# V of all four head pairs as one product of 512 columns, in two passes over the contraction

## The chip, the cores and the metric

The kernel runs on one core of a Trainium2 chip. The metric is device time in microseconds (us) of one execution, the median of three runs. The engines named below are TensorE (PE, with its weight loads PEld), VectorE (DVE), ScalarE (ACT), GpSimd (POOL) and SyncE (SP). Each takes its own instructions strictly in order and waits for the others by semaphores. DMA transfers are issued from the queues of SP and ACT.

## The reference

One decoder layer over 2048 positions of 1024 channels, in float32. Its first step is a projection of x; the rest is attention, a state-space branch (S5), gates, an output projection and a layer norm.

```python
proj = jnp.einsum('bld,de->ble', h, w_in[layer])
q, k, v   # 3 groups x 8 heads x 64 each, = 1536 columns each
z_a, u_s, z_s   # 512 columns each
gate_logits     # 2048 columns
attn = _dilated_mixture(q, k, v)        # per group: band of 128 keys back, dilation 1, 4, 16
attn = attn * silu(z_a);  y_a = attn @ w_attn_up
y = gelu(_s5(u_s, ...)); y = y * sigmoid(y @ w_glu + b_glu) * silu(z_s); y_s = y @ w_ssm_up
out = (sigmoid(g_a) * y_a + sigmoid(g_s) * y_s) @ w_o
h = layer_norm(ALPHA * h + out)
```

## The kernel before

Every float32 product is made of three products of parts: x and each weight are split into a high part (a cast to fp32r, "hi") and the rest ("lo"), and hi·hi, hi·lo and lo·hi are summed in PSUM. So one block of 128 output channels over 1024 positions is 8 tiles of the contraction x 2 halves of the positions x 3 = 48 matmuls of 512 columns. The sequence is done in two halves of 1024 positions (h = 0, 1).

**Weights.** `Weights` walks along a list of weight tiles, 128 x 1024 each. `fetch` issues the load of a tile (on ACT's queue, L137). `ahead` and `ahead2` are called inside the block that uses the tile before: they split the next tile in two parts of 512 columns, hi by a cast on ACT (L172), lo by a subtraction on POOL (L175; for some later tiles on DVE), and fetch the one after it. `take` hands a tile to its block.

**Jobs.** A job is one head pair (of four) in one of three groups. `job_proj` makes its V, Q and K; Q and K are one block each (`xgemm`, L215). V is made for two head pairs at once, in jobs of even pairs: `v_gemm` (L431 on) has x as the stationary operand and 256 weight columns as the moving one, 192 matmuls (L446). Two groups of four tiles of positions use two PSUM banks of the tag `proj`; the first half of the contraction is done for all four tiles, then the second half with the second weight tile. Each full bank is copied to SBUF by ACT (L414, tile `th`) and stored to DRAM (`vD`, L415). The job of the odd pair finds its V there.

**Attention.** `job_attn` (L534 on) is a chain over eight tiles of positions. One step has scores on PE (L595, L597), a sum with the bias and a row extreme on DVE (L602), exponentials on ACT (L606), transposes of the tile before on PE (L614), their split by ACT (L616) and DVE (L617), the product with V of the tile before that (L625), and sums by ACT (L630), DVE (L632) and POOL (L633).

**Order.** The instructions stand in the order in which the program writes them. `interleave` runs the projections of the next job (the bulk, in units of six matmuls) beside the attention of the last one (the side), each at its share of a given total. A bulk is counted in blocks of 48 matmuls of 512 columns: four blocks for a job with V, three for a job of an odd pair (Q, K and one further block, za or zs). The four u blocks stand at the start of each half.

Of the kernel before, what the change touches and what calls it, by code (L numbers as in the profile page):

```python
# [41 lines left out]
def layer_kernel(ctx, tc, xT, xnat, w_in, w_v, w_up, w_glu, w_o, bglu, lng, lnb,  # L42
# [30 lines left out]
    vD = [[[dram.tile([HALF, 256], F32, name=f"vD{h}{p}{g}") for g in range(3)] for p in range(2)] for h in range(2)]  # L73
# [49 lines left out]

    class Weights:
# [14 lines left out]
        def load_first(self, i, k):  # L139
            c = self.cols(i, k)  # L140
            S.dma_start(self.raws[i][0][:, c], self.plan[i][:, c])
# [13 lines left out]
        def begin(self):  # L155
            raw, n = self.raws[len(self.splits)]
            left = len(self.plan) - len(self.splits)
            if left <= 4:
                hi, lo = (mpbox["mp"].tile([128, HALF], F32R, name=f"w{n_}", tag=f"m{2 * left - 1 - k_}")
                          for k_, n_ in enumerate(("hi", "lo")))  # L160
            else:
                hi = wp.tile([128, HALF], F32R, name="whi", tag="whi", bufs=2)
                lo = wp.tile([128, HALF], F32R, name="wlo", tag="wlo", bufs=2)
            self.splits.append((hi, lo))
            self.part(0)

        def part(self, k, i=None):
            i = len(self.splits) - 1 if i is None else i
            hi, lo = self.splits[i]
            raw = self.raws[i][0]  # L170
            c = self.cols(i, k)
            A.copy(hi[:, c], raw[:, c])  # L172

            def low(eng):
                eng.tensor_tensor(lo[:, c], raw[:, c], hi[:, c].bitcast(F32), op=OP.subtract)  # L175
# [99 lines left out]
    def first_blocks(load, evac):  # L275
# [22 lines left out]
        for kt, blk in order:  # L298
            if blk == 0 and kt < 7:
                next(load)  # L300
            if (kt, blk) == (0, 0):
                for i in range(2):
                    wts.part(1, i)
            mms(blk, kt)
            if (kt, blk) == (2, 1):
                wts.fetch(4)
            yield 6 * 0.216
            if (kt, blk) == (7, 0):
                wts.ahead()
                wts.finish()  # L310
                for t in range(2):
                    evac[0](t, ps[0][t])
# [51 lines left out]
    def job_proj(ap, wts, h, pair, g):  # L364
# [9 lines left out]
        odd = pair % 2  # L374
        vd = vD[h][pair // 2][g]

        def load_v():

            c = slice(128 * odd, 128 * odd + 128)
# [51 lines left out]
    def v_gemm(evac):  # L431
        w = [wts.take(), None]
        wts.ahead()
        for grp in range(2):
            ps = [ps_tile("proj", 2).rearrange("t (i c) -> t i c", i=2) for _ in range(2)]
            for half_k in range(2):
                if grp == 0 and half_k == 1:
                    w[1] = wts.take()
                for t in range(4):
                    o = ps[t // 2][:, t % 2]  # L440
                    for k4 in range(4):
                        kt = 4 * half_k + k4
                        wc = slice(k4 * 256, (k4 + 1) * 256)
                        for n, (m, wx) in enumerate((("h", 0), ("h", 1), ("l", 0))):
                            i = 4 * grp + t
                            T.matmul(o, X[m, kt][:, 128 * i:128 * i + 128], w[half_k][wx][:, wc],  # L446
                                     start=kt == 0 and n == 0 and t % 2 == 0, stop=kt == 7 and n == 2,
                                     skip_group_check=True)
                    if (grp, half_k) in ((0, 0), (1, 1)):
                        if t == 0:  # L450
                            wts.ahead()
                            if grp == 0:
                                wts.finish()
                        if t == 1:
                            wts.ahead2()
                    if half_k and t % 2:
                        evac(2 * grp + t // 2, ps[t // 2])
                    yield 6 * 0.216
# [215 lines left out]
    def u_evac(h, b):  # L674
        def ev(t, ps):
            ut = wp.tile([128, 512], F32, name="th", tag="th", bufs=2)
# [15 lines left out]
    def z_block(dst, outer=False):  # L692
# [5 lines left out]
        def ev(t, ps):  # L698
            zt[t] = wp.tile([128, 512], F32, name="th", tag="th", bufs=2)
# [7 lines left out]
    def gate_block(h, d, outer=False, early=False):  # L707
        box = {}

        def ev(t, ps):  # L710
            cols = slice(t * 512, (t + 1) * 512)
            if early:
                zt = wp.tile([128, 512], F32, name="th", tag="th", bufs=2)
# [9 lines left out]

    plan = []
    for h in range(2):
        plan += [w_in[40 + b] for b in range(4)]
        for pair in range(NPAIR):
            for g in range(3):
                if pair % 2 == 0:
                    plan += [w_v[pair // 2, g, k] for k in range(2)]  # L730
                plan += [w_in[12 * m + g * 4 + pair] for m in range(2)]
                if pair % 2:
                    plan.append((w_in[36 + pair - 1], w_in[44 + pair // 2], w_in[36 + pair])[g])
# [225 lines left out]
    with tc.tile_pool(name="ap", bufs=1) as ap:  # L959
        ub = [u_block(0, b) for b in range(2, 4)]  # L960
        interleave(chain([first_blocks(first_x(ap), [u_evac(0, b) for b in range(2)])] + ub
                         + [job_proj(ap, wts, 0, 0, 0)]), 8 * BLK, s5_tables(ap), 32.0)
        table_store.pop()()
        pend = None
        for h in range(2):
            bulk = [u_block(1, b, b == 0) for b in range(4)] if h else []
            n = len(bulk)
            for pair in range(NPAIR):
                for g in range(3):
                    if h or pair or g:  # L970
                        bulk.append(job_proj(ap, wts, h, pair, g))
                        n += 2 if pair % 2 else 4
                    if pair % 2:
                        bulk.append(zs_block(h, pair // 2) if g == 1 else za_block(h, pair - 1 + g // 2))
# [3 lines left out]
                    else:  # L978
                        interleave(chain(bulk), n * BLK, pend, 16.0, 12 * 0.216 if g == 0 and pair % 2 else 0.0)
# [273 lines left out]
    def stage_glu(h, sact, stile, zs):  # L1253
        late = []

        def ev_e(e, box):
            def ev(t, ps):
# [3 lines left out]
                th = wp.tile([128, 512], F32, name="th", tag="th", bufs=2)  # L1261
# [359 lines left out]
def host_layout(inp):  # L1621
# [11 lines left out]
    wv = a["w_in"][0][:, 3072:4608].reshape(2, 4, 128, 3, 2, 256)  # L1633
    d["w_v"] = c(wv.transpose(4, 3, 0, 2, 1, 5).reshape(2, 3, 2, 128, 1024))
# [40 lines left out]
```

## Time and profile before

| | |
|---|---|
| median of three runs | 2167.19 us (2167.11 to 2167.34) |
| the profiled execution's own time | 2166.73 us |
| its span, first to last instruction | 2164.9 us |
| PE busy | 2137.0 us, 99% |
| DVE, ACT, POOL busy | 55%, 47%, 33% |
| granted TensorE clock, mean | 0.998 |

A line of the profile names the engine, the line of the program, the operation, what it writes and reads, and its duration. Matmuls overlap: each is shown for longer than the time to the next one's start, so rates are read from starts that follow each other. In brackets stands how long the engine was idle before, and which instruction it waited for.

### The profile page before, as it was taken

How to read it: one execution, taken by the hardware profiler on the slowest of the kernel's cores; microseconds unless marked ns; L12 is line 12 of the kernel's file. 1: busy time of each engine (PE TensorE's matmuls, PEld its weight loads, DVE VectorE, ACT ScalarE, POOL GpSimd, SP SyncE). 2: the span in 40 equal slices, each digit the busy share in tenths (PEclk: the TensorE clock that was granted, in tenths of full speed). 3: DMA queues.
4: the chain of work that ended last, by engine and by line, in shares of the span. 5: the costliest groups of instructions: out<-in, count | busy, mean ns of one | idle time of the engine just before them, and what ended most of it. 6: DMA issues, size and time to landing. Idle time of an engine off the chain costs nothing. (4 is left out here: it accounts for less than half of the span.)

```text
span 2164.9 us, 32185 instructions
## 1 busy us (share of the span) xinstructions
PE 2137.0 (99%) x11440; PEld 1822.8 (84%) x11440; DVE 1191.7 (55%) x3062; ACT 1007.4 (47%) x2355; POOL 704.2 (33%) x589
## 2 busy tenths in 40 slices
PE   8999999999999999999999999999999999999998
PEld 7998889998888999889998888888888878888786
DVE  7644554445553244554445654258887784358725
ACT  3355665556554355665555665233433352232222
POOL 2322253253342234243243252410100014322643
PEclk9999999999999999999999999999999999999999
DMA  6333344343374333434344344554345363533721
GB/s 177 112 98 96 108 127 128 95 127 118 104 233 97 97 99 122 124 108 113 97 130 117 106 108 119 175 169 142 112 141 166 124 208 127 159 114 118 261 88 78
DMA packets 227568, 278.12 MB, mean 128 GB/s; under 512 B 89552, under 2 KB 175440, under 8 KB 227408
## 3 DMA queue, kind: packets, MB, share of 16 engines
q10 hardware_dynamic: 91776, 143.81, 21.7%
q1 hardware_dynamic: 135632, 132.25, 20.6%
q8 instruction: 91, 1.49, 0.3%
q14 instruction: 69, 0.57, 0.1%
HBM read 189.24 MB, written 74.19 MB: 122 GB/s over the span
## 5 line engine op out<-in xcount | busy, mean ns | idle before, releaser
L215 PE MATMUL proj<-xh,whi 128*128 128x512 f32 x1600 | 645.1, 403 | 1.2 <-ACT gt L719 1.2
L215 PE MATMUL proj<-xh,wlo 128*128 128x512 f32 x1600 | 628.2, 393 | 0.0
L215 PE MATMUL proj<-xl,whi 128*128 128x512 f32 x1600 | 625.8, 391 | 0.0
L175 POOL TENSOR_TENSOR wlo<-wraw,whi 128x512 fp32r<-128x512 f32 (+1 forms) x268 | 357.1, 1343 | 530.7 <-ACT whi L172 508.9
L215 PEld LDWEIGHTS proj<-xh,wlo 128*128 128x128 f32 x1600 | 300.2, 188 | 65.5
L215 PEld LDWEIGHTS proj<-xh,whi 128*128 128x128 f32 x1600 | 301.4, 188 | 54.6 <-issue 1.5
L215 PEld LDWEIGHTS proj<-xl,whi 128*128 128x128 f32 x1600 | 301.2, 188 | 51.3
L606 ACT ACTIVATE Sx<-Sx,st 128x256 f32<-128x256 f32 (+1 forms) x384 | 181.3, 473 | 263.8 <-DVE st L602 254.9
L633 POOL TENSOR_TENSOR og<-ot 128x128 f32<-128x128 f32 x192 | 88.1, 459 | 532.7 <-DVE ot L632 516.4
L172 ACT CAST whi<-wraw 128x512 fp32r<-128x512 f32 (+1 forms) x328 | 194.7, 617 | 116.5 <-PE ob L1406 43.2
L617 DVE TENSOR_TENSOR PT<-tr,PT 128x512 fp32r<-128x512 f32 (+1 forms) x192 | 118.9, 619 | 219.9 <-ACT PT L616 219.7
L446 PE MATMUL proj<-whi,xh 128*128 128x256 f32 x768 | 220.8, 287 | 0.0
L446 PE MATMUL proj<-wlo,xh 128*128 128x256 f32 x768 | 218.1, 284 | 0.9 <-POOL wlo L175 0.8
L446 PE MATMUL proj<-whi,xl 128*128 128x256 f32 x768 | 217.1, 283 | 0.0
L446 PEld LDWEIGHTS proj<-wlo,xh 128*128 128x128 f32 x768 | 146.7, 191 | 2.9 <-POOL wlo L175 2.4
L446 PEld LDWEIGHTS proj<-whi,xl 128*128 128x128 f32 x768 | 146.7, 191 | 0.0
L446 PEld LDWEIGHTS proj<-whi,xh 128*128 128x128 f32 x768 | 146.6, 191 | 0.1
L602 DVE CUSTOM_DVE_ANT_0 Sx<-sca,bias 128x256 f32<-128x256 f32 (+1 forms) x192 | 74.6, 389 | 105.3 <-PE sca L597 101.8
L632 DVE TENSOR_TENSOR ot<-ob,ot 64x256 f32<-64x256 f32 x192 | 81.0, 422 | 83.3 <-ACT ot L630 71.7
L632 DVE TENSOR_TENSOR ot<-oa,ot 64x256 f32<-64x256 f32 x192 | 81.1, 422 | 75.1 <-ACT ot L630 61.9
L614 PE MATMUL tr<-ident,Sx 128*128 128x128 f32 x664 | 110.0, 276 | 5.7 <-ACT Sx L606 5.1
L400 DVE TENSOR_TENSOR KC<-proj,KC 64x512 fp32r<-64x512 f32 x96 | 66.1, 689 | 82.9 <-ACT KC L398 81.6
(319 smaller groups left out, 3778.9 us busy)
## 6 DMA issues: line engine op xcount, KB each, us to landing
wraw<-in_w_in_dram ACTq DMA_DIRECT2D x102, 512.0 KB
ld<-gD SPq DMA_DIRECT2D x32, 512.0 KB
gD<-gt ACTq DMA_DIRECT2D x27, 512.0 KB
wraw<-in_w_v_dram ACTq DMA_DIRECT2D x24, 512.0 KB
vD<-th ACTq DMA_DIRECT2D x48, 256.0 KB
cB<-coefD SPq DMA_DIRECT2D x48, 256.0 KB
VV<-vD SPq DMA_DIRECT2D x16, 512.0 KB
xr<-in_xT_dram SPq DMA_DIRECT2D x16, 512.0 KB
```

The costliest lines, as they stand in the source:

```text
L172: A.copy(hi[:, c], raw[:, c])
L175: eng.tensor_tensor(lo[:, c], raw[:, c], hi[:, c].bitcast(F32), op=OP.subtract)
L215: T.matmul(ps, w[:, wc], m(kt)[:, cols], start=kt == 0 and n == 0, stop=3 * kt + n == last)
L400: V.tensor_tensor(gdst(lo, g, t), gsrc(ps[rows[s]], g), gdst(hi[rows[s]].bitcast(F32), g, t), op=OP.subtract)
L446: T.matmul(o, X[m, kt][:, 128 * i:128 * i + 128], w[half_k][wx][:, wc], start=kt == 0 and n == 0 and t % 2 == 0, stop=kt == 7 and n == 2, ...
L602: V.tensor_tensor_reduce(sx[:, s, lo:], ps2[s][:, lo:256], bias[:, s, lo:], scale=-0.125, scalar=3.0e38, op0=OP.add, op1=OP.min, accum_out ...
L606: A.activation(sx[:, s, lo:], sx[:, s, lo:], AF.Exp, scale=-1.0, bias=st[:, 0, s, c:c + 1], accum_out=st[:, 1, s, c:c + 1])
L614: T.transpose(p3[:, s, b], Sx[i][:, s, b * 128:(b + 1) * 128], ident)
L617: V.tensor_tensor(PT[:, 1, :, pos], p3[:, :, lo:], PT[:, 0, :, pos].bitcast(F32), op=OP.subtract)
L632: V.tensor_tensor(ot[half[s]], O[half[s], s], ot[half[s]], op=OP.add)
L633: P.tensor_tensor(og[pair, g][:, i * 128:(i + 1) * 128], ot[:, 0], ot[:, 1], op=OP.add)
```

## The change

V of a group is now made for all four head pairs at once, in the jobs of pair 0: 512 weight columns are the moving operand, and one matmul does what two did. A weight tile now holds two tiles of the contraction instead of four, so a V product needs four weight tiles. It goes in two passes, each over half the contraction: in pass 0 each group of two position tiles is copied to `th` by ACT and stored to DRAM; in pass 1 that sum is loaded again, added to the bank by DVE and stored. These stores and loads are issued by SP. The two PSUM banks of a group are now filled alternately and both are full at the group's end.

Weight tiles are held in pieces of 512 columns: three pieces of raw weights instead of two tiles of 1024, four pieces each of hi and lo as before in bytes. Each piece has its own load. `th` has three buffers instead of two. The first two weight tiles lie in a tile that V uses later.

Of the four u blocks of half 0, two remain at the start (u2 and u3 go beside attention); of those of half 1, one remains. za, zs and u blocks now stand one by one in the jobs of pairs 1 to 3 by the table `BESIDE`; only job (3, 1) of half 0 has none.

```diff
-                raw = wp.tile([128, HALF], F32, name="wraw", tag="wraw", bufs=2)
-                if len(self.raws) > 2:
-                    A.dma_start(raw[:, :n], src)
+                raw = Split()
+                for p in range(2):
...
+                        raw.tiles[p] = wp.tile([128, 512], F32, name="wraw", tag="wraw", bufs=3)
+                        A.dma_start(raw.tiles[p], src[:, 512 * p:512 * p + 512])
...
-        def ev_v(b, ps):
-            vs = wp.tile([128, 512], F32, name="th", tag="th", bufs=2).rearrange("k (i c) -> k i c", i=2)
-            A.copy(vs, ps)
-            A.dma_start(vd[256 * b:256 * b + 256].rearrange("(i k) c -> k i c", i=2), vs)
-        if not odd:
-            yield from v_gemm(ev_v)
+        if not pair:
+            yield from v_gemm(vd)
...
+        def load(grp):
+            for tt in range(2 * grp, 2 * grp + 2):
+                S.dma_start(tile_of(tt), rows(tt))
+        for p in range(2):
+            w = [wts.take(), None]
+            wts.ahead()
+            if p:
+                load(0)
+            for grp in range(4):
+                ps = [ps_tile("proj", 2) for _ in range(2)]
+                for k4 in range(4):
+                    if grp == 0 and k4 == 2:
+                        w[1] = wts.take()
+                    wc = slice(512 * (k4 % 2), 512 * (k4 % 2) + 512)
+                    for t in range(2):
+                        i = 2 * grp + t
+                        for n, (m, wx) in enumerate((("h", 0), ("h", 1), ("l", 0))):
+                            T.matmul(ps[t], X[m, 4 * p + k4][:, 128 * i:128 * i + 128], w[k4 // 2][wx][:, wc],
+                                     start=k4 == 0 and n == 0, stop=k4 == 3 and n == 2)
+                    if (grp, k4) == (0, 0):
+                        wts.finish()
+                    if (grp, k4) == (0, 1):
+                        wts.ahead2()
+                    if grp == 3 and k4 == 0:
+                        wts.ahead()
+                    if grp == 3 and k4 == 1:
+                        wts.ahead2()
+                    if k4 == 3:
+                        for t in range(2):
+                            tt = 2 * grp + t
+                            if p:
+                                V.tensor_tensor(vs[tt], ps[t], vs[tt], op=OP.add)
+                            else:
+                                A.copy(tile_of(tt), ps[t])
+                            S.dma_start(rows(tt), vs[tt])
+                        if p and grp < 3:
+                            load(grp + 1)
                     yield 6 * 0.216
...
+    BESIDE = {(1, 0): "a0", (1, 1): "u2", (1, 2): "s0", (2, 0): "a1", (2, 1): "u3", (2, 2): "s1", (3, 0): "a2",
+              (3, 2): "a3"}
+    extra = [BESIDE, {**BESIDE, (3, 1): "u1"}]
+    front = [2, 1]
```

On PE, at the start of the V product of job (0, 1) of half 0, before the change: behind the scores stand 48 matmuls with the first weight tile (whi_1049), two groups of 12 in bank proj_1144 and two in proj_1145, then the second weight tile (whi_1140).

```order
L597 MATMUL scb_1122<-KC_603,QLb0_600 128x128
L446 MATMUL proj_1144<-whi_1049,xh0_191 128x256
...
L446 MATMUL proj_1145<-whi_1049,xh0_191 128x256
...
L614 MATMUL tr_1209<-ident_71,Sx_1127 128x128 x2
L446 MATMUL proj_1144<-whi_1140,xh4_275 128x256
L446 MATMUL proj_1144<-wlo_1141,xh4_275 128x256
```

The same place on PE after the change (whi_1022 and whi_1038 are the two pieces of the first weight tile, whi_1117 is the first piece of the second):

```order
L639 MATMUL scb_1099<-KC_391,QLb0_388 128x128
L480 MATMUL proj_1121<-whi_1022,xh0_186 128x512
L480 MATMUL proj_1121<-wlo_1023,xh0_186 128x512
L480 MATMUL proj_1121<-whi_1022,xl0_187 128x512
L480 MATMUL proj_1122<-whi_1022,xh0_186 128x512
...
L480 MATMUL proj_1122<-whi_1038,xl1_203 128x512
L480 MATMUL proj_1121<-whi_1117,xh2_238 128x512
L480 MATMUL proj_1121<-wlo_1118,xh2_238 128x512
```

The second weight tile is now the 13th matmul instead of the 49th, and the second bank the 4th instead of the 25th.

On ACT, at the same place before the change: the casts of the last K block, the exponentials of the first attention step, then both hi casts of the second weight tile.

```order
L398 CAST KC_603<-proj_1079 64x4x128 x2
L606 ACTIVATE Sx_1127,st_1118<-Sx_1127,st_1118 128x128 x2
L172 CAST whi_1140<-wraw_1067 128x512 x2
L137 DMA wraw_1172<-in_w_in_dram 128x1024
```

And after it:

```order
L425 CAST KC_391<-proj_1056 64x4x128 x2
L648 ACTIVATE Sx_1104,st_1095<-Sx_1104,st_1095 128x128 x2
L198 CAST whi_1117<-wraw_1042 128x512
L198 CAST whi_1129<-wraw_1044 128x512
L153 DMA wraw_1139<-in_w_v_dram 128x512
L153 DMA wraw_1141<-in_w_v_dram 128x512
```

The hi casts stand at the same place on ACT as before; only what needs them on PE has moved.

On DVE, at the end of the first group of pass 1 of the same V product, after the change (before, no V work stood on DVE): the sums of an attention step (sca_1379, scb_1380), the split of its transposes (tr_1390), then the two adds that empty the banks proj_1351 and proj_1352. "ISA" is what the profile calls CUSTOM_DVE_ANT_0.

```order
L644 ISA Sx_1385,st_1095<-sca_1379,bias_1092 128x256
...
L659 TENSOR_TENSOR PT_1096<-tr_1390,PT_1096 128x2x256
L494 TENSOR_TENSOR th_1347<-proj_1351,th_1347 128x512
L494 TENSOR_TENSOR th_1349<-proj_1352,th_1349 128x512
```

On PE there, the scores and the transposes stand ahead of the last unit of six, and the next group (proj_1411, in the bank of proj_1351) follows directly:

```order
L637 MATMUL sca_1379<-KC_391,QA_385 128x256
...
L656 MATMUL tr_1390<-ident_71,Sx_1302 128x128 x4
L480 MATMUL proj_1351<-whi_1359,xh7_333 128x512
...
L480 MATMUL proj_1411<-whi_1278,xh4_278 128x512
```

## Rows read from the trace of the kernel before

**Rows 1.** The page: busy us (share of the span) and instructions of engines.

```profile
PE 2137.0 (99%) x11440; PEld 1822.8 (84%) x11440; DVE 1191.7 (55%) x3062; ACT 1007.4 (47%) x2355; POOL 704.2 (33%) x589
```

**Rows 2.** The page, one of V's three product groups: count, busy, mean ns, idle.

```profile
L446 PE MATMUL proj<-wlo,xh 128*128 128x256 f32 x768 | 218.1, 284 | 0.9 <-POOL wlo L175 0.8
```

**Rows 3.** Timeline of PE: start, us, engine, line; steady stretches of both products.

```profile
31.11 0.39 PE L215 MATMUL proj<-xh,whi 128*128 128x512 f32 x1
33.83 0.39 PE L215 MATMUL proj<-xh,whi 128*128 128x512 f32 x1
...
57.30 0.28 PE L446 MATMUL proj<-wlo,xh 128*128 128x256 f32 x1
60.90 0.28 PE L446 MATMUL proj<-wlo,xh 128*128 128x256 f32 x1
```

**Rows 4.** Timeline, start of the V product of job (0, 1), half 0.

```profile
97.90 1.18 ACT L398 CAST KC<-proj 64x512 fp32r<-64x512 f32 x2 [3.20 <-PE proj L215]
98.09 0.33 PE L446 MATMUL proj<-whi,xh 128*128 128x256 f32 x1
99.11 1.39 DVE L400 TENSOR_TENSOR KC<-proj,KC 64x512 fp32r<-64x512 f32 x2 [4.03 <-ACT KC L398]
102.18 1.13 ACT L172 CAST whi<-wraw 128x512 fp32r<-128x512 f32 x2
102.92 2.56 POOL L175 TENSOR_TENSOR wlo<-wraw,whi 128x512 fp32r<-128x512 f32 x2 [3.74 <-issue]
104.50 0.37 PE L446 MATMUL proj<-whi,xh 128*128 128x256 f32 x1
```

**Rows 5.** Timeline, three other V products: PE's first matmul, POOL's lo.

```profile
52.87 0.28 PE L446 MATMUL proj<-whi,xh 128*128 128x256 f32 x1
55.00 2.58 POOL L175 TENSOR_TENSOR wlo<-wraw,whi 128x512 fp32r<-128x512 f32 x2 [6.33 <-ACT whi L172]
...
750.91 0.28 PE L446 MATMUL proj<-whi,xh 128*128 128x256 f32 x1
755.99 2.54 POOL L175 TENSOR_TENSOR wlo<-wraw,whi 128x512 fp32r<-128x512 f32 x2 [6.10 <-ACT whi L172]
...
807.49 0.28 PE L446 MATMUL proj<-whi,xh 128*128 128x256 f32 x1
813.07 2.53 POOL L175 TENSOR_TENSOR wlo<-wraw,whi 128x512 fp32r<-128x512 f32 x2 [2.58 <-issue]
```

**Rows 6.** Timeline, end of a u block that fills both banks alternately.

```profile
667.58 0.58 ACT L678 COPY th<-proj 128x512 f32<-128x512 f32 x1 [0.34 <-PE proj L215]
667.84 0.40 PE L215 MATMUL proj<-xh,wlo 128*128 128x512 f32 x1
668.22 0.50 PE L215 MATMUL proj<-xh,whi 128*128 128x512 f32 x1
```

**Rows 7.** Timeline, scores and transposes in a row in an attention step.

```profile
131.47 0.28 PE L595 MATMUL sca<-KC,QA 128*128 128x256 f32 x1
131.95 0.60 PE L614 MATMUL tr<-ident,Sx 128*128 128x128 f32 x4
133.50 0.56 ACT L616 CAST PT<-tr 128x512 fp32r<-128x512 f32 x1
134.09 0.69 DVE L617 TENSOR_TENSOR PT<-tr,PT 128x512 fp32r<-128x512 f32 x1 [1.29 <-ACT PT L616]
```

**Rows 8.** Windows, attention (0,0) beside four blocks, (1,0) beside three: us, busy.

```profile
97.70:153.70 56.00, 56.00 (x382) 51.59 (x381) 24.27 (x67) 30.71 (x77) 17.02 (x19) 1.00 0.27 81
250.70:295.50 44.80, 44.75 (x238) 37.32 (x237) 26.70 (x77) 28.47 (x74) 15.99 (x16) 1.00 0.31 87
```

**Rows 9.** Timeline of PE: the matmuls behind the longest wait.

```profile
1769.54 0.79 PE L215 MATMUL proj<-yh,whi 128*128 128x512 f32 x1 [4.18 <-ACT th L1263]
1770.56 0.63 PE L215 MATMUL proj<-yh,wlo 128*128 128x512 f32 x1
1770.98 0.63 PE L215 MATMUL proj<-yh,whi 128*128 128x512 f32 x1
```

More of the change, by code (lines that the diff above doesn't have):

```diff
@@ L72, in layer_kernel @@
     tabD = dram.tile([128, 1472], F32, name="tabD")
-    vD = [[[dram.tile([HALF, 256], F32, name=f"vD{h}{p}{g}") for g in range(3)] for p in range(2)] for h in range(2)]
+    vD = [[dram.tile([HALF, 512], F32, name=f"vD{h}{g}") for g in range(3)] for h in range(2)]
     zaD = [[dram.tile([128, HALF], F32, name=f"zaD{h}{p}") for p in range(NPAIR)] for h in range(2)]
@@ L121, in next_x, with __init__, __getitem__ @@
         split_x(7, raws[7])
+    class Split:
+        def __init__(self):
+            self.tiles = {}
+        def __getitem__(self, key):
+            rows, c = key
+            p = c.start // 512
+            return self.tiles[p][rows, c.start - 512 * p:c.stop - 512 * p]
     class Weights:
@@ L157, in begin @@
             left = len(self.plan) - len(self.splits)
+            pair = Split(), Split()
             if left <= 4:
[L159 to L164, printed above, removed]
+                for k_, n_ in enumerate(("hi", "lo")):
+                    t = mpbox["mp"].tile([128, HALF], F32R, name=f"w{n_}", tag=f"m{2 * left - 1 - k_}")
+                    for p in range(2):
+                        pair[k_].tiles[p] = t[:, 512 * p:512 * p + 512]
+            self.splits.append(pair)
             self.part(0)
@@ L170, in part @@
             raw = self.raws[i][0]
-            c = self.cols(i, k)
-            A.copy(hi[:, c], raw[:, c])
+            cuts = self.cuts(i, k)
+            for c in cuts:
+                p = c.start // 512
+                if p not in hi.tiles:
+                    hi.tiles[p] = wp.tile([128, 512], F32R, name="whi", tag="whi", bufs=4)
+                    lo.tiles[p] = wp.tile([128, 512], F32R, name="wlo", tag="wlo", bufs=4)
+                A.copy(hi[:, c], raw[:, c])
             def low(eng):
-                eng.tensor_tensor(lo[:, c], raw[:, c], hi[:, c].bitcast(F32), op=OP.subtract)
+                for c in cuts:
+                    eng.tensor_tensor(lo[:, c], raw[:, c], hi[:, c].bitcast(F32), op=OP.subtract)
             if i in self.late:
@@ L429, in job_proj @@
         jobs.append(j)
[L431 to L443, printed above, removed]
-                        for n, (m, wx) in enumerate((("h", 0), ("h", 1), ("l", 0))):
[L445 to L457, printed above, removed]
@@ L675, in ev @@
         def ev(t, ps):
-            ut = wp.tile([128, 512], F32, name="th", tag="th", bufs=2)
+            ut = wp.tile([128, 512], F32, name="th", tag="th", bufs=3)
             u3 = ut.rearrange("c (p n) -> c p n", p=16)
@@ L959, in layer_kernel @@
     with tc.tile_pool(name="ap", bufs=1) as ap:
-        ub = [u_block(0, b) for b in range(2, 4)]
-        interleave(chain([first_blocks(first_x(ap), [u_evac(0, b) for b in range(2)])] + ub
-                         + [job_proj(ap, wts, 0, 0, 0)]), 8 * BLK, s5_tables(ap), 32.0)
+        wts.first = ap.tile([128, 2 * HALF], F32, name="w01", tag="VV", bufs=2)
+        interleave(chain([first_blocks(first_x(ap), [u_evac(0, b) for b in range(2)])] + [job_proj(ap, wts, 0, 0, 0)]), 8 * BLK, s5_tables(ap), 32.0)
         table_store.pop()()
@@ L965, in layer_kernel @@
         for h in range(2):
-            bulk = [u_block(1, b, b == 0) for b in range(4)] if h else []
+            bulk = [u_block(1, b, b == 0) for b in range(front[1])] if h else []
             n = len(bulk)
@@ L978, in layer_kernel @@
                     else:
-                        interleave(chain(bulk), n * BLK, pend, 16.0, 12 * 0.216 if g == 0 and pair % 2 else 0.0)
+                        interleave(chain(bulk), n * BLK, pend, 16.0, 12 * 0.216 if (pair, g) == (1, 0) else 0.0)
                     pend = job_attn(ap, jobs.pop())
```

55 lines of the change are left out of this document (37 added, 18 removed).

## The prediction

> **What bounds the kernel now.** The first view is the table of engines [rows 1]: PE is busy 99% of the span and no other engine above 55%. So the end is set by how fast PE's queue runs, and a change pays by what it takes out of that queue, and costs what it makes PE wait. The second view is the costliest groups [rows 2]: a V product of 256 columns stands there 768 times in each of three groups, 2304 in all, and PE hardly waited ahead of them (0.9 us in that group, 0.8 of them for POOL's lo). The shown durations overlap, so the rate is read from the timeline, as the distance of starts [rows 3]: 12 matmuls of 512 columns from 31.11 to 33.83 us are 0.2267 us each, 30 of 256 columns from 57.30 to 60.90 are 0.1200 each. Two small ones take 0.2400, more than one large one.
>
> **What the change takes away.** 2304 x 0.1200 = 276.5 us become 1152 x 0.2267 = 261.1 us: -15.4 us. Attention beside them is the same on both sides. This term is as sure as the two rates; it is the whole gain.
>
> The Trainium skill (TensorE: Matmul & The Clock Gate, section Back-to-back issue gap) gives the spacing of a warm matmul as columns / 2.4 + 2.5 ns, that is 109 ns for 256 columns and 216 for 512. By that the gain would be only 251.6 - 248.6 = 3 us. The starts [rows 3] differ from it (120 and 227 ns), and the measured ones decide.
>
> **The second weight tile comes too late.** In a V product that runs beside attention, PE before used the first weight tile for 48 matmuls of 256 columns, 5.8 us, and the second stood ready just in time [rows 4]: the V product starts at 98.09; ACT casts the last K bank until 99.08, DVE subtracts until 100.50, then come the bias and the sums of the first attention step and ACT's exponentials, and only at 102.18 the two hi casts of the second weight tile. POOL's two lo pieces take 2.56 us from 102.92, so the first is done at 104.20, 6.11 us after the start; PE reached it at 104.50. The order of ACT, DVE and POOL there is not changed, but PE now gets to that lo piece after 12 matmuls of 512 columns and one with hi: 2.72 + 0.23 = 2.95 us. It waits 6.11 - 2.95 = 3.16 us. (Part of this wait is met earlier, at the 4th matmul: its bank is that of the last K block, which DVE gives back at 100.50, 2.41 us after the start, where PE needs it after 0.68. It is the same time and is not counted twice.)
>
> The other products of V by the same reckoning: job (0, 2) of half 0 stands in the same order, 3.16. In half 1 the first lo ends 1.27 us after 755.99, 6.35 after the start at 750.91, and 6.85 after the start at 807.49 [rows 5]: waits of 3.40 and 3.90. The first V product of a half has no attention step ahead; there the first lo ends 3.42 us after the start [rows 5], a wait of 0.47, and I take this for both halves. Sum 2 x 3.16 + 3.40 + 3.90 + 2 x 0.47 = +14.6 us. Ends: 1 us if ACT could cast right behind the K bank (99.08 + 0.6 + 1.28 is 2.9 us after the start), 18 if the second piece is late as well. In the order of ACT the exponentials stand ahead of the casts, so I take the full value.
>
> In pass 1 the same wait is shorter: the fourth tile's hi cast stands behind two bank copies of 0.58 us [rows 6] and two small ones, and its lo behind a small sum on POOL; by these it is ready some 4 us after the pass begins and wanted at 3. I take 1.0 us in the five products with attention, +5.0; ends 0 and 3.2 each (as in pass 0), so 0 and 16.
>
> **The ends of groups.** There are 48 groups of two banks, and both banks of each are full only at its end; the next group needs the first at once. The trace has one such place, a u block that fills both banks alternately [rows 6]: its last matmul starts at 667.84, ACT copies the first bank from 667.58 to 668.16, and the next block's first matmul starts at 668.22, 0.38 after 667.84 instead of 0.23. So a bare end costs 0.15 us with ACT's copy; with DVE's add, which I take at the 0.69 us of a DVE operation of 512 columns that reads PSUM [rows 7], 0.25. In the order of PE, 24 of the 48 ends have no attention product behind them to cover this (all 8 of the first V product, 3 in each of four, 4 in the first of half 1). In five of these 24, scores and transposes stand ahead of the group's last unit, and DVE has to do that step's sums and split before the add. How long that takes is seen where scores and transposes followed each other before [rows 7]: from the scores at 131.47 to the end of DVE's split, 134.09 + 0.69, are 3.31 us. The add ends 4.0 us after the scores, while PE is through scores, transposes and the six matmuls after 0.48 + 0.44 + 1.36 = 2.28: a wait of 1.7. Sum 5 x 1.7 + 19 x 0.2 = +12.3 us. Ends: 3.6 (24 bare ends of 0.15) and 20 (five more of the long kind).
>
> The Trainium skill (same page, section Loop structure matters more than you think) counts the copy out of PSUM as free: the next iteration's matmuls follow immediately. By that this term would be 0 and the sum 12.3 lower. The row at 668.22 [rows 6] speaks against it for two banks that fill together.
>
> **The blocks dealt out anew.** The count of blocks is the same, but three jobs of each half, those of pair 2, lose their V and become jobs of three blocks. An attention chain beside three blocks is denser, and PE waits more for it [rows 8]: beside four, 56.0 us less 192 x 0.1200 and 96 x 0.2267 leave 11.2; beside three, 44.8 less 144 x 0.2267 leave 12.2 for the same form of attention. Six jobs x 1.0 = +6.0 us. Ends: 0, and 12 (job (3, 1) of half 0 has two blocks only, where ACT's 28.47 us of work and DVE's 26.70 would meet a PE time of about 34).
>
> **What I cost at nothing.** 48 adds on DVE (33 us) and the split weight loads on ACT lie beside PE's work, with DVE at 55% and ACT at 47%. In pass 1 a sum is loaded one group, 5.4 us, ahead of its add; the trace before has no such load. A weight piece now waits in ACT's queue for the lo of an earlier piece, and exponentials stand behind it. These together: 0, ends -1 (V's 48 stores leave ACT's queue) and +10.
>
> **Sum**, against the profiled execution of 2166.7 us: -15.4 + 14.6 + 5.0 + 12.3 + 6.0 = +22.5, so 2189.2; the median of the runs lies 0.5 above the profiled one, so **2190 us**. With its ends this case is 2177 to 2204.
>
> **Rivals.**
> *Faster:* the stream's gain stands and PE's waits are filled, because attention products cover the group ends and the casts come early enough. For it: PE waits almost nowhere before, with eviction and splitting always hidden. Against it: the lo of the second tile was ready 0.3 us before it was wanted [rows 4], with twice the time. Bare ends alone: 2166.7 - 15.4 + 3.6 = 2155 us.
> *No change:* only the second tile's wait comes; while PE stands, ACT, DVE and POOL catch up, so the ends of groups and the denser jobs cost nothing: -15.4 + 14.6 = 2166 us, with what is left of bare ends up to 2172. For it: each wait lets the chain behind it run ahead. Against it: the long ends of groups lie 10 us and more after that wait.
> *Much slower, by the clock:* PE's longest wait before, 4.18 us, was followed by matmuls 0.43 us apart instead of 0.23 [rows 9], the level of 1.2 GHz instead of 2.4. If the waits of three microseconds bring this too, at some 1.6 us each time (0.36 + 6 x 0.2), ten of them add 16: 2206 us. Against it: most are split in two by the bank's wait.
> *The change doesn't do what it says:* 512 columns of weights as the moving operand run no better than the small ones. Then the gain falls from 15.4 to about 3 or less, and the sum is 2202 us. Against it: L215 has the same shape and runs at 0.2267.
>
> **How the numbers follow.** Chances: the forecast 0.57, faster 0.17, no change 0.13, the clock 0.10, no gain from the shape 0.03. The rival without change splits into 0.08 within 0.2% (4.3 us, about what a measurement of this kernel can tell from no change) and 0.05 slower. So faster 0.17, same 0.08, slower 0.57 + 0.05 + 0.10 + 0.03 = 0.75. The range of 2160 to 2207 takes in the forecast's own 2177 to 2204, the case of no change and the upper edge of the faster one, and leaves out some 0.17.
>
> **What would show it.** V products 0.227 us apart confirm the first term. In job (0, 1) PE should wait for DVE's K subtraction at the 4th and for POOL's lo at the 14th V matmul, together 3 us; in pass 1 about 1 us at the 14th. At ends of groups PE should wait for ACT's copy or DVE's add, 0.15 to 0.25 us, and 1.7 behind scores and transposes. The forecast is wrong if the lo of the second tile is ready within 3 us of a V product's start, or if PE's waits in V add up to less than 15 us.

## The result and the profile after

The changed kernel takes 2219.38 us (median of four runs, 2217.73 to 2220.78) against 2167.27 of the kernel before on the same chip: ratio 1.0238, interval 1.0225 to 1.025. It is slower by 52 us; the forecast was slower by 23, and the range ended at 2207. The profiled span grew from 2164.9 to 2215.8 us.

The page of the changed kernel, to be read beside [rows 1, 2]:

```profile
PE 2145.2 (97%) x10288; PEld 1757.3 (79%) x10288; DVE 1213.8 (55%) x3110; ACT 1011.6 (46%) x2357; POOL 706.7 (32%) x591
L480 PE MATMUL proj<-whi,xh 128*128 128x512 f32 x384 | 157.0, 409 | 17.1 <-DVE th L494 8.7
L480 PE MATMUL proj<-wlo,xh 128*128 128x512 f32 x384 | 151.7, 395 | 8.2 <-POOL wlo L202 8.2
L242 PE MATMUL proj<-xh,whi 128*128 128x512 f32 x1600 | 646.5, 404 | 11.9 <-DVE th L494 10.7
```

PE fell from 99% to 97%: the new time is waiting. 1152 matmuls fewer are issued, and V's waits, 0.9 us in one group before, are now 17.1 and 8.2; a third sum, 11.9, stands ahead of the blocks that `xgemm` makes (L242, Q and K among them), and 10.7 of it is a wait for DVE's add (L494).

To place the waits, I take on PE the distance between the starts of two matmuls, less the steady distance of the first one's shape (0.2267 or 0.1200 us), and add it up by place over the whole trace. From the first matmul to the last the changed kernel is 51.5 us longer:

| term | forecast | measured |
|---|---|---|
| stream, 1152 x 0.2267 for 2304 x 0.1200 | -15.4 | -15.4 |
| second weight tile and second bank, pass 0 | +14.6 | +16.6 |
| second weight tile, pass 1 | +5.0 | +5.2 |
| other waits in V (ends of groups), less the 6.4 that V had before | +12.3 | +16.1 |
| first Q block behind the first V product | 0 | +10.0 |
| other waits up to the first attention step (mostly low clock) | 0 | +2.0 |
| blocks dealt anew | +6.0 | +14.8 |
| S5 stage and all behind it | 0 | +2.2 |

The rows of the terms that came as forecast, on the timeline of the changed kernel (start, us, engine, line; in brackets the engine's idle time and what ended it):

```profile
59.66 0.39 PE L480 MATMUL proj<-whi,xl 128*128 128x512 f32 x1
61.70 0.39 PE L480 MATMUL proj<-whi,xl 128*128 128x512 f32 x1
...
114.31 0.44 PE L480 MATMUL proj<-whi,xh 128*128 128x512 f32 x1
116.86 0.47 PE L480 MATMUL proj<-whi,xh 128*128 128x512 f32 x1 [1.64 <-DVE KC L427]
119.04 0.50 PE L480 MATMUL proj<-whi,xh 128*128 128x512 f32 x1
119.12 2.51 POOL L202 TENSOR_TENSOR wlo<-wraw,whi 128x512 fp32r<-128x512 f32 x2 [3.72 <-issue]
120.44 0.50 PE L480 MATMUL proj<-wlo,xh 128*128 128x512 f32 x1 [0.90 <-POOL wlo L202]
...
149.10 0.60 PE L656 MATMUL tr<-ident,Sx 128*128 128x128 f32 x4
150.70 0.40 PE L480 MATMUL proj<-whi,xl 128*128 128x512 f32 x1
151.25 0.69 DVE L659 TENSOR_TENSOR PT<-tr,PT 128x512 fp32r<-128x512 f32 x1 [1.29 <-ACT PT L658]
151.85 0.68 DVE L494 TENSOR_TENSOR th<-proj,th 128x512 f32<-128x512 f32 x1
152.59 0.50 PE L480 MATMUL proj<-whi,xh 128*128 128x512 f32 x1 [1.49 <-DVE th L494]
152.93 0.40 PE L480 MATMUL proj<-wlo,xh 128*128 128x512 f32 x1
```

Nine distances from 59.66 to 61.70 are 0.2267 each. Job (0, 1)'s V product begins at 114.31, waits for the K bank at its 4th matmul and for POOL's lo at its 14th (120.44); the first of POOL's two lo pieces ends some 6.1 us after the start, as in [rows 4]. At 152.59 stands the long end behind scores and transposes: DVE's split first, then the add, and PE 1.66 us late. The second matmul of the group follows 0.34 behind the first (152.93) instead of 0.23.

And the rows of what was not foreseen, DVE and PE beside the first V product:

```profile
62.31 0.69 DVE L494 TENSOR_TENSOR th<-proj,th 128x512 f32<-128x512 f32 x1 [9.67 <-DMA th<-vD]
77.64 1.29 DVE L973 COPY PT<-arena 64x32 f32<-64x32 f32 x1
80.23 0.39 PE L480 MATMUL proj<-whi,xl 128*128 128x512 f32 x1
88.64 0.94 DVE L847 TENSOR_SCALAR PT<-arena 64x288 f32<-64x288 f32 x3
89.61 1.29 DVE L494 TENSOR_TENSOR th<-proj,th 128x512 f32<-128x512 f32 x2
90.45 0.77 PE L242 MATMUL proj<-xh,whi 128*128 128x512 f32 x1 [9.84 <-DVE th L494]
91.02 0.63 PE L242 MATMUL proj<-xl,whi 128*128 128x512 f32 x1
```

DVE works there on the tables of S5 (`s5_tables`, L973 among others). It stood idle for 9.67 us before the first sum: the add is next in its queue, PE's product for it is complete only at about 61.4 us, and its load ends the wait at 62.3. Later the last add stands behind 12 us of table code, from 77.64 to 89.58, and the first Q block waits for its bank until 90.45.

### The profile page after: what moved, and what is told of

Its sections match the earlier page's. It is cut to its first block, busy times and chain, and to the rows that moved or that the text cites. A ratio compares the mean times of both kernels' runs of the same rounds, so it can differ in the third digit from the quotient of the medians.

```text
span 2215.8 us, 30577 instructions
## 1 busy us (share of the span) xinstructions
PE 2145.2 (97%) x10288; PEld 1757.3 (79%) x10288; DVE 1213.8 (55%) x3110; ACT 1011.6 (46%) x2357; POOL 706.7 (32%) x591
## 4 chain that ended last, share of the span: by engine, by line
PE 61%; ACT 4%; DVE 3%; issue 2%; POOL 1%; ACTq 0%; DMA 0%; POOLq 0%; DVEq 0%; SPq 0%
PE proj L242 31%; PE proj L1399 8%; PE proj L480 5%; PE proj L1457 2%; PE tr L1457 2%; PE tr L656 2%; ACT Sx L648 1%; PE oa L667 1%; PE sca L1457 1%; PE scb L1457 1%; PE oa L1457 1%; PE ob L1457 1%; PE ob L667 1%; POOL wlo L202 1%; DVE KC L427 1%
## 5 line engine op out<-in xcount | busy, mean ns | idle before, releaser
L242 PE MATMUL proj<-xh,whi 128*128 128x512 f32 x1600 | 646.5, 404 | 11.9 <-DVE th L494 10.7
L242 PE MATMUL proj<-xh,wlo 128*128 128x512 f32 x1600 | 629.0, 393 | 0.0
L242 PE MATMUL proj<-xl,whi 128*128 128x512 f32 x1600 | 626.4, 391 | 0.0
L202 POOL TENSOR_TENSOR wlo<-wraw,whi 128x512 fp32r<-128x512 f32 x266 | 352.2, 1336 | 548.7 <-ACT whi L198 395.8
L242 PEld LDWEIGHTS proj<-xh,whi 128*128 128x128 f32 x1600 | 301.9, 189 | 65.2 <-issue 13.3
L242 PEld LDWEIGHTS proj<-xh,wlo 128*128 128x128 f32 x1600 | 300.6, 188 | 66.0
L242 PEld LDWEIGHTS proj<-xl,whi 128*128 128x128 f32 x1600 | 301.6, 189 | 51.0
L198 ACT CAST whi<-wraw 128x512 fp32r<-128x512 f32 x324 | 192.6, 617 | 118.4 <-PE ob L1457 37.1
L480 PE MATMUL proj<-whi,xh 128*128 128x512 f32 x384 | 157.0, 409 | 17.1 <-DVE th L494 8.7
L480 PE MATMUL proj<-wlo,xh 128*128 128x512 f32 x384 | 151.7, 395 | 8.2 <-POOL wlo L202 8.2
L480 PE MATMUL proj<-whi,xl 128*128 128x512 f32 x384 | 151.0, 393 | 0.0
L658 ACT CAST PT<-tr 128x512 fp32r<-128x512 f32 (+1 forms) x192 | 99.6, 519 | 25.2 <-PE tr L656 14.0
L480 PEld LDWEIGHTS proj<-whi,xh 128*128 128x128 f32 x384 | 72.1, 188 | 45.7 <-DVE th L494 13.7
L656 PEld LDWEIGHTS tr<-ident,Sx 128*128 128x128 f32 x664 | 79.1, 141 | 27.0 <-ACT Sx L648 15.1
L672 ACT COPY ot<-ob 64x256 f32<-64x256 f32 x192 | 70.6, 368 | 52.9 <-PE ob L667 47.4
```

Of the source, the lines that this page charges most:

```text
L242: T.matmul(ps, w[:, wc], m(kt)[:, cols], start=kt == 0 and n == 0, stop=3 * kt + n == last)
L480: T.matmul(ps[t], X[m, 4 * p + k4][:, 128 * i:128 * i + 128], w[k4 // 2][wx][:, wc], start=k4 == 0 and n == 0, stop=k4 == 3 and n == 2)
L656: T.transpose(p3[:, s, b], Sx[i][:, s, b * 128:(b + 1) * 128], ident)
L658: A.copy(PT[:, 0, :, pos], p3[:, :, lo:])
```

## The experiments

All ratios are to the kernel before, run on the same chip; each experiment edits the changed kernel.

**Finer tables.** The loop that ends in 12 us of one piece hands over at each step:

```diff
             V.tensor_copy(Q2[64:128, :, jj], wr[64:128, :, 7 - jj])
+            yield 0.25
...
-        yield 2.0
```

> The loop of the table code that runs on DVE beside the first V product hands over after each of its 8 steps instead of once at its end; nothing else differs from the changed kernel. Theory A (the 10.2 us gap ahead of the first Q block is the last sum of the first V product, queued on DVE behind 12 us of table code): that gap shrinks to under 1.5 us and the time falls by 9 to 10 us, to about 2210. Rival (the sum waits for its load from DRAM or its store, and the table code only fills the time): the gap stays and the time is 2217 to 2220.

2218.2 us, ratio 1.023 (1.0215 to 1.0245). Theory A failed on the time, and so did the rival on the gap. The gap at the first Q block fell from 10.0 to 1.8 us, and a new one of 7.8 came at the first K block:

```profile
93.50 0.39 PE L242 MATMUL proj<-xh,wlo 128*128 128x512 f32 x1
99.81 0.25 DVE L847 TENSOR_SCALAR PT<-PT 128x128 f32<-128x128 f32 x1
99.97 0.68 DVE L427 TENSOR_TENSOR QLa<-proj,QA 64x512 fp32r<-64x512 f32 x1
100.66 0.69 DVE L427 TENSOR_TENSOR QLb<-proj,QB 64x512 fp32r<-64x512 f32 x1
101.50 0.76 PE L242 MATMUL proj<-xh,whi 128*128 128x512 f32 x1 [7.62 <-DVE QLb L427]
```

Q's own subtraction comes right behind the end of the table code. So it is not one add alone that is late. That all of DVE's queue is behind, by the time that it stood idle, is what the pacing below puts to the test.

**V in the old shape, blocks in the new deal.** `v_gemm` makes two products of 256 columns over the whole contraction, one behind the other, with no sums in DRAM:

```diff
+        for p in range(2):
+            yield from v_half(vd, p)
+    def v_half(vd, p):
...
+                    for k4 in range(4):
+                        kt = 4 * half_k + k4
+                        wc = slice(k4 * 256, (k4 + 1) * 256)
...
+                        A.copy(vs, ps[t // 2])
+                        S.dma_start(vd[256 * b:256 * b + 256, 256 * p:256 * p + 256]
+                                    .rearrange("(i k) c -> k i c", i=2), vs)
```

> The changed kernel's deal of blocks, but V again in products of 256 columns over the whole contraction, two of them one behind the other in the job of pair 0, with no sums in DRAM. Theory A (V's 512-column form itself brings 47.8 us of waits against a saving of 15.4, and the new deal of blocks the rest): 2219.4 - 47.8 + 15.4 = 2187, that is about 20 above the kernel before. Rival B (the new deal costs the 6 us of the forecast and nothing else): 2173. Rival C (the waits come from having all of V ahead of one job, whatever its shape): above 2200.

2182.37 us, ratio 1.0068 (1.0053 to 1.0083): 14.8 above the kernel before, 37.0 below the changed one. B and C fall; A, at 2187, is 5 high. V's waits are 6.5 us here, as before. So all of the change but V's new form costs 14.8, and V's new form 37.0, its gain of 15.4 included. The deal of blocks is not alone in these 14.8: the weight pieces and the three buffers of `th` are in them too.

**No sums.** The second pass copies and stores like the first; loads and additions are left out, and with them the first half of the contraction.

```diff
-                            if p:
-                                V.tensor_tensor(vs[tt], ps[t], vs[tt], op=OP.add)
-                            else:
-                                A.copy(tile_of(tt), ps[t])
+                            A.copy(tile_of(tt), ps[t])
                             S.dma_start(rows(tt), vs[tt])
-                        if p and grp < 3:
-                            load(grp + 1)
```

> The second pass leaves out the loads of the first pass's sums and the additions: ACT copies and stores as in the first pass, so V holds only the second half of the contraction. Theory A (the sums through DRAM cost the 10.2 us behind the table code, some 2.4 us of late loads in the first V product, and part of the 1.7 us ends behind scores and transposes): 2200 to 2207. Rival (an end of a group costs the same whether ACT copies or DVE adds, and the 10.2 us are something else's): 2216 to 2220.

2201.95 us, ratio 1.0155 (1.014 to 1.0171): 17.4 less, as theory A has it. The waits up to the first attention step fall by 12.0; each of the five other V products gains 0.7 to 1.9. So the sums cost something everywhere, and most of it beside the tables. This run takes out the loads and the adds together and does not tell them apart.

**Second tile early.** The first half of the second tile is split in the last quarter of the block ahead, and for the second pass in the last group of the first:

```diff
+                if (t, kt) == (1, 3) and lead:
+                    wts.early()
...
+                    if grp == 3 and k4 == 2 and not p:
+                        wts.early()
```

> The first half of V's second weight tile is split (cast on ACT, subtracted on POOL) already in the last quarter of the block ahead of V, into the buffers that this block has done with; in pass 1 a quarter of a group earlier; nothing else differs from the changed kernel. Theory A (PE's waits at the 13th and 14th V matmul, 8.4 us in the first and 5.2 in the second passes, are the lateness of this tile): they go, and the time falls by 10 to 14 us, to about 2207. Rival (the tile's second half, or the banks, end the same wait a little later): 2214 to 2220.

2213.85 us, ratio 1.0211 (1.0194 to 1.0228): 5.5 less, half of what theory A says. By the view of V's line, which adds up the idle time of PE and of its weight loads (so one wait can count twice), POOL's share of V's waits falls from 20.4 to 3.6 us, but ACT's bank copies now come to 16.3 instead of 7.5. The rows of the cured place, and of the new wait in job (0, 2):

```profile
118.17 0.40 PE L492 MATMUL proj<-whi,xl 128*128 128x512 f32 x1
120.21 0.47 PE L492 MATMUL proj<-whi,xh 128*128 128x512 f32 x1 [1.65 <-DVE KC L439]
122.37 0.39 PE L492 MATMUL proj<-whi,xh 128*128 128x512 f32 x1
...
228.93 0.49 PE L492 MATMUL proj<-whi,xh 128*128 128x512 f32 x1 [1.56 <-ACT th L510]
```

The 13th matmul starts at 122.37 and the 14th follows 0.23 behind it: PE runs through the second tile without a stop. At the start of the second pass it waits for ACT: the early cast stands ahead of the last group's copy in ACT's queue and is itself held up there, in job (0, 2) by the load of its raw weights (1.30 us idle), in the first V product by PE (2.27 us).

**Bank by bank.** In groups 1 to 3 all 12 matmuls of one bank run before the other's:

```diff
+                units = ([(k4, t) for k4 in range(4) for t in range(2)] if grp < 1
+                         else [(k4, t) for t in range(2) for k4 in range(4)])
```

> In groups 1 to 3 of each pass the 12 matmuls of the first bank run before the 12 of the second, instead of six and six alternately; group 0 stays as it is; nothing else differs from the changed kernel. Theory A (a group's end costs because both banks become full together): about 12 us of V's 43 us of waits stand at the ends of these groups and at the second bank's start, and go; the time is 2207 to 2212. Rival (the ends cost because ACT or DVE come late, whichever bank is first): 2217 to 2221.

2224.85 us, ratio 1.0261 (1.0245 to 1.0277): 5.5 more. Both sides missed. The ends of groups 1 and 2 in the first passes do vanish (0.16 us at the next group's first matmul and 0.11 at its second), but the second passes, whose group 0 alternates, now wait at their 4th matmul for the copy of the bank that was filled last:

```profile
146.86 0.50 PE L481 MATMUL proj<-whi,xh 128*128 128x512 f32 x1 [0.98 <-ACT th L495]
```

That is 0.8 to 1.4 us in five products.

**A third block for the short job.** The first gate block of half 0 moves from the S5 stage to job (3, 1) of half 0, which has two blocks:

```diff
-    extra = [BESIDE, {**BESIDE, (3, 1): "u1"}]
+    extra = [{**BESIDE, (3, 1): "g0"}, {**BESIDE, (3, 1): "u1"}]
```

> In half 0 the job of pair 3, group 1, which has only the Q and K blocks, gets a third block: the first gate block of half 0, taken from the later S5 stage; nothing else differs from the changed kernel. Theory A (that job is too short for its attention chain: 5.7 and 5.5 us of waits stand in it and behind it, against 1.7 and 2.3 in other jobs): 6 to 8 us go, if the S5 stage loses nothing by the missing block; 2211 to 2214. Rival (the waits in it are not a matter of its length, or the S5 stage needs that block as cover): 2217 to 2221.

2218.11 us, ratio 1.0235 (1.0217 to 1.0253): 1.3 less, no more than the noise, and inside the rival's range. The windows of the changed kernel (attention beside the two-block job, the one behind it, the rest from the S5 stage on; us, PE busy, PEld, DVE, ACT, POOL, granted clock, DMA share, GB/s), and then of this one:

```profile
581.10:618.90 37.80, 34.87 (x191) 28.73 (x190) 23.72 (x72) 25.55 (x69) 10.21 (x12) 1.00 0.29 85
618.90:665.70 46.80, 44.08 (x225) 35.88 (x224) 26.46 (x72) 27.84 (x74) 28.45 (x23) 1.00 0.55 152
1357.50:2206.80 849.30, 841.68 (x3769) 688.67 (x3767) 526.35 (x1171) 288.40 (x543) 216.11 (x148) 1.00 0.46 144
```

```profile
581.30:626.10 44.80, 44.74 (x239) 37.37 (x238) 26.65 (x78) 28.48 (x74) 15.99 (x16) 1.00 0.32 93
626.10:669.90 43.80, 43.11 (x226) 35.95 (x225) 23.62 (x66) 27.13 (x73) 25.29 (x19) 1.00 0.56 161
1361.60:2205.40 843.80, 831.18 (x3721) 679.13 (x3719) 524.06 (x1169) 285.42 (x539) 210.60 (x148) 1.00 0.46 144
```

The two jobs take 88.6 us instead of 84.6 with 48 matmuls (10.9 us) more: 6.9 gained, as theory A has it. The S5 stage and what follows lose the same 10.9 us of work and get only 5.5 shorter: 5.4 given back, as the rival has it. Each side was right about its half.

**Tables paced.** The pieces of table code get other weights, so that more of it stands ahead of the first sum. Two versions were run; the first cut line below is in both, the last two are of the second version, which hands over to the first sum before the power n = 4:

```diff
         expo(dt, prm["ld"])
-        yield 3.0
+        yield 2.0
...
+            yield (0.1, 0.0, 2.0, 0.0, 0.1)[n]
...
+            yield 1.2 if jj == 4 else 0.2
```

> The table code on DVE is cut into finer pieces and handed over so that about 10 us more of it stand ahead of the first sum of the first V product, and the rest is spread between the sums; nothing else differs from the changed kernel. In the changed kernel DVE stood idle for 9.7 and 2.4 us in front of the first two sums while table code waited behind them, and with finer pieces alone the wait moved from the first Q block to the first K block. Theory A (DVE's queue loses these 12 us at the sums, and the 57 us of table code then end too late for whatever is queued behind): the idle time goes, and the time falls by 8 to 11 us, to about 2209. Rival (table code and sums together are more than DVE can do beside the first V product, whatever their order): PE waits elsewhere and the time is 2214 to 2220.

> The table code beside the first V product is paced once more, now by the trace: about 62 us into the execution DVE should reach the first sum, with some 4 us of table code between two sums; nothing else differs from the changed kernel. With 6 us too much ahead of the first sum the wait only moved there (5.7 us), and DVE stood idle later. Theory A (only the order of DVE's queue is at fault; DVE has room for tables and sums beside the first V product): the waits from the first V product's second pass to the first K block, 14 to 16 us so far, shrink to 4 to 6, and the time is 2208 to 2212. Rival (the room is not there): 2216 to 2220.

First version: 2218.65 us, ratio 1.0231 (1.0213 to 1.025). Too much code stood ahead of the first sum, and the wait moved there:

```profile
62.93 0.39 PE L480 MATMUL proj<-whi,xl 128*128 128x512 f32 x1
67.91 0.69 DVE L494 TENSOR_TENSOR th<-proj,th 128x512 f32<-128x512 f32 x1
68.66 0.79 PE L480 MATMUL proj<-whi,xh 128*128 128x512 f32 x1 [5.34 <-DVE th L494]
```

Second version: 2212.35 us, ratio 1.0205 (1.019 to 1.022), 7.0 less than the changed kernel and at the edge of what theory A gives. DVE now has no more than about half a microsecond of idle time ahead of each of the four pairs of sums, instead of 9.67 ahead of the first:

```profile
61.85 1.29 DVE L494 TENSOR_TENSOR th<-proj,th 128x512 f32<-128x512 f32 x2
68.11 1.29 DVE L494 TENSOR_TENSOR th<-proj,th 128x512 f32<-128x512 f32 x2 [0.53 <-issue]
73.96 1.37 DVE L494 TENSOR_TENSOR th<-proj,th 128x512 f32<-128x512 f32 x2 [0.50 <-PE proj L480]
81.81 1.29 DVE L494 TENSOR_TENSOR th<-proj,th 128x512 f32<-128x512 f32 x2
```

PE's waits up to the first attention step fall from 21.9 to 14.1 us, by 7.8 of the 12.0 that leaving out the sums took away there. So the order of DVE's queue, with the same work in it, made most of that loss.

**Early tile and order by banks, and all together.** The early split for the first pass alone, and another order inside groups; then the same with the paced tables:

```diff
+                cut = ((0, 3, 4), (0, 2, 4))[p] if grp == 0 else (0, 4, 4)
+                units = [(k4, t) for a, b in zip(cut, cut[1:]) for t in range(2) for k4 in range(a, b)]
```

> Two changes to the changed kernel: the first half of the second weight tile of the first pass is split during the block ahead of V, and within a group the matmuls are ordered by bank: in group 0 of the first pass 9 matmuls for one bank, 9 for the other, 3 and 3, in that of the second pass 6, 6, 6 and 6, in all other groups 12 and 12. Theory A (the waits in V are a matter of what is wanted first: the bank that the K block gives back late, the tile that is split late, the sum behind a scores step): 8 us of bank waits and 8 of tile waits in the first passes, and some 7 us of the ends behind scores in the second passes go; 2196 to 2206. Rival (each moved demand meets another late engine, as bank by bank alone did): 2212 to 2224.

> The paced table code, the early tile and the order by banks together. Theory A (the three act on different waits and add up): 2186 to 2198, still 20 and more above the kernel before, because the deal of blocks alone costs 15. Rival (the first V product stays bound by DVE, and the moved demands meet other engines): 2210 to 2220.

Without the pacing 2211.55 us, ratio 1.0199 (1.0182 to 1.0216), above the range of theory A and just below that of the rival: the five V products beside attention lose 8.9 us of their waits, but at the first K block 7.3 us of DVE's lateness come up again. With it 2194.75 us, ratio 1.0125 (1.011 to 1.0141): 24.6 less than the changed kernel, inside the range. The two cures need each other: together they give 24.6, alone 7.0 and 7.8. V still waits 32.1 us, and POOL's lo is the largest part: of the 16.1 us that PE itself shows idle ahead of V's matmuls, 11.8 end with it. No version beats the kernel before. With 14.8 for the rest of the change against the stream's 15.4, a gain would be left only if V waited less than 7 us, hardly more than the 6.4 before.

## Why the prediction was wrong

The direction was right, and so were four of its steps. The stream's gain is 15.4. The second tile's wait is 16.6 for 14.6 forecast, in the two halves that the step names; the first V product is the one place off, with 2.2 for 0.47. Pass 1 costs 5.2 for 5.0.

At the ends of groups the five behind scores and transposes measure 1.0 to 1.7 us, two others 1.1 and 1.3, the bare ones 0.15 to 0.3: 12.8 at the groups' first matmuls, for 12.3. The term came out 16.1 mostly because behind each such wait the group's second matmul comes 0.11 late as well (152.93 above), which was not counted; the second bank's first matmul, the 4th, is on time. Behind the row that the step was read from, 668.22 in [rows 6], the next start is at 668.55, late by the same 0.1. The Trainium skill (TensorE: Matmul & The Clock Gate, section Loop structure matters more than you think) lets the next matmuls follow a copy out of PSUM at once; for two banks that fill together the bare ends of 0.15 us and more speak against it, as [rows 6] did.

The step that failed is "48 adds on DVE (33 us) and the split weight loads on ACT lie beside PE's work, with DVE at 55% and ACT at 47%". It used the mean over the span for a stage with another load, and put at nothing what cost PE 12.0 us there. This window of the kernel before shows it (columns as above):

```profile
0.00:97.70 97.70, 91.83 (x480) 79.10 (x481) 71.41 (x254) 31.73 (x47) 26.80 (x24) 1.00 0.54 152
```

DVE was busy for 71.4 of 97.7 us up to the first attention step, most of it with table code in one queue. PE did not feel it, as u blocks and V were copied out by ACT. The change put adds into this queue, which wait in order for a load and for PE, and everything behind them waits too. That is 10.0 us at the first Q block and 2.0 around it; the 10.0 stand at the last end of the first V product, one of the 24 ends that the forecast had at 0.2. Without the sums the 12.0 are gone, and with DVE's queue in another order 7.8 of them. The step's own end of +10 came near; its value in the sum was nothing.

The second miss is a size: "Six jobs x 1.0 = +6.0 us", with 12 as the end. The experiment with the old shape gives 14.8. By jobs in its trace, the two-block job and the one behind it have 11.5 us of waits where the same pair has 4.3 with the third block, the other new three-block jobs about 1.2 each, near the forecast, and the stage from S5 on 2.1 more (together some 16.5, the difference of the two traces). The text named the two-block job, but only for the upper end: the six jobs of its sum are those of pair 2, so job (3, 1) stands there at nothing. Moving a block there regained 6.9, so its length was the cause of those. That the table's 14.8, which leaves out the stage from S5 on, equals the 14.8 of this run, which has it, is chance.

The stage from S5 on, 2.2 us, was in no term. Nearly all of it is one place, the longest wait of [rows 9]: 6.08 us instead of 4.18, and 8 matmuls 0.43 apart behind it instead of 6. The changed kernel there:

```profile
1817.12 2.55 ACTq L153 DMA_DIRECT2D wraw<-in_w_up_dram  x2
1819.71 0.69 ACT L1314 ACTIVATE th<-proj,bgl_h 128x512 f32<-128x512 f32 x1 [3.98 <-DVE wlo L202]
1820.45 0.80 PE L242 MATMUL proj<-yh,whi 128*128 128x512 f32 x1 [6.08 <-ACT th L1314]
```

Two loads of weight pieces stand in ACT's queue ahead of the activation that frees PE's bank, and wait for the lo of earlier pieces; before, it was one load. The step that failed put these split loads at nothing too. The run with the old shape keeps them, and has the wait at 6.06 us. But ACT's own idle time there grew only from 3.38 to 3.98, so how much of the 1.9 us is theirs is not shown.

The range was too narrow by the prediction's own numbers. Its upper ends add up to 18 + 16 + 20 + 12 + 10 - 15.4 = 60.6 us, which is 2228, and its lower ends to 2155; "2177 to 2204" follows from neither, and no working is given for it. The measured 2219 lies inside the ends and outside the range.

Of the rivals, *faster* and *no change* needed ends and deal to be free, and they were not. *The change doesn't do what it says* is out by the 0.2267. *The clock* came true in one new place only: behind the longest wait, 9.84 us, the matmuls start 0.42 apart (91.02 on). The waits of 1.4 to 1.7 us in the V products beside attention have no such row behind them: behind 116.86 the distance is 0.30 once and then 0.23.

What stays open: the rest of that wait in the S5 stage, and the 14.1 us that remain up to the first attention step with the second pacing. Of these 5.9 lie in V, and 8.2 outside it, where the kernel before had 4.2. They were not taken apart further.

## What to carry to other kernels

An engine's mean share over the span says nothing on the stage in which new work lands: take the window of that stage, and ask what stands in the queue before and behind the new instruction. An instruction that waits in its queue for a load holds up all that stands behind it, and the loss can show far from the wait: 9.67 us of idle DVE at 62 us were 10.0 us of waiting PE at 80. When a wait is cured and the time stays, look for the same microseconds a block further on before dropping the theory.

## What was not expected of the hardware

The granted clock fell after one long wait and after a short one in the same place of another kernel. The windows (columns as above) behind the wait of 9.84 us in the changed kernel and, below it, behind one of 2.18 us with the second pacing:

```profile
90.40:95.00 4.60, 4.55 (x13) 3.69 (x14) 4.28 (x29) 0.00 (x0) 0.00 (x0) 0.63 0.34 124
```

```profile
82.60:85.50 2.90, 2.86 (x7) 2.31 (x8) 2.80 (x11) 0.00 (x0) 1.74 (x2) 0.50 0.76 242
```

A granted clock of 0.50 is the level of 1.2 GHz, for all of the second window's 2.9 us; 0.63 is a mix of both levels. The length of the wait alone does not tell whether the clock falls. The wait of V's 4th matmul in job (0, 1) shows both: behind 1.64 us at 116.86 in the changed kernel the next matmuls start 0.30 and then 0.23 apart, and in the run with the third block they come to 0.43 apart behind 1.65 us:

```profile
115.33 0.47 PE L480 MATMUL proj<-whi,xh 128*128 128x512 f32 x1 [1.65 <-DVE KC L427]
116.23 0.63 PE L480 MATMUL proj<-whi,xh 128*128 128x512 f32 x1
116.66 0.63 PE L480 MATMUL proj<-wlo,xh 128*128 128x512 f32 x1
```

What else decides was not tried.

Single DVE copies of 64x32 that take 0.19 us elsewhere took 1.2 to 1.3 now and then, as L973 at 77.64. In the changed kernel it is 4 of 24, 4.1 us of the 12 us of table code ahead of the last sum, and all four fall while POOL makes a lo (77.64 and 78.94 in the first row, 82.24 and 83.42 in the second):

```profile
77.30 2.82 POOL L202 TENSOR_TENSOR wlo<-wraw,whi 128x512 fp32r<-128x512 f32 x2 [17.18 <-ACT whi L198]
82.04 2.53 POOL L202 TENSOR_TENSOR wlo<-wraw,whi 128x512 fp32r<-128x512 f32 x2 [1.92 <-ACT whi L198]
```

So the two go together here; no experiment took POOL's work away, so that it is the cause is not shown.
